# A hybrid scan and convolution layer: the scan's levels 1 to 3 multiplied in one visit, levels 4 to 6 in the last, and convolution operands stored in one run per partition

## The chip, the cores and the metric

The kernel runs on one core of one Trainium2 chip. The metric is the device time of one execution in microseconds (us); the kernel before takes 2150.0 us, the median of three runs (2148.01 to 2152.14). A core has TensorE (PE, with its weight loads PEld), VectorE (DVE), ScalarE (ACT), GpSimd (POOL) and SyncE (SP), which here only issues DMAs. Each engine works through its own queue in order, and engines wait for one another by semaphores.

## What is computed

One layer over 2048 tokens of width 1024, with 256 context tokens ahead of it. A normalised input is multiplied by one large matrix. Part of the result feeds eight heads of a gated linear recurrence that runs in both directions, part a gated convolution of width three along rows of 64 tokens; both are joined and multiplied by an output matrix.

```python
def chunk_scan(q, k, v, logf, s0):
    # S_t = diag(f_t) S_{t-1} + k_t v_t^T,  o_t = S_t^T q_t
    ...
    attn = jnp.einsum('bhtk,bhsk,bhtsk->bhts', qc, kc, decay)
    o = einsum(attn, vc) + einsum(qc * jnp.exp(bcum), S)
...
p = h @ w_in[l]
o, _, _ = bidir_scan(q, kf, kb, v, gf, gb, s_f, s_b)
y_hg = hgrn_out(o, p[..., 4 * HG_WIDTH:HG_COLS], hg_onorm_w[l], x.dtype)
y_cv = conv_branch(p[..., HG_COLS:], conv_w[l], grid=True)
y = jnp.concatenate([y_hg, y_cv], axis=-1) @ w_out[l]
x = x + gate[:, None] * y
```

`decay` is the product of the gates f between two tokens of a chunk.

## The kernel before

**Wide products.** Every large product is done with f16 pairs (a high and a low part, three matmuls for one) and by Strassen's scheme in Winograd's form, `seven`: seven half-size products with operands named B11, T1, T2, B21, T3, B22, T4. Their matmuls are lines 930 to 932. One such product for one stretch of tokens is a "unit". In the head stage a unit covers 512 tokens and its matmuls have 256 columns; in the pair stage, where convolution blocks 1 to 7 are computed, a unit covers 1024 tokens and its matmuls have 512 columns.

**Stages in order.** First the input is normalised (to about 100 us). Then 32 windows follow, eight heads by four token groups of 512, each with two or three units (until about 1265 us). Four windows of the first convolution block come next, then 14 windows of the pair stage (from about 1340 us), and last the output product (from about 1845 us).

**The scan.** The projections of one window are scanned in the next; the scan of one head and group is a "segment" (`Seg`), so there are 32. Q and K hold queries and keys for both directions. The attention within a chunk of 128 is built by levels: at level `lev`, tokens are in blocks of B = 2^lev, and only pairs of neighbouring blocks are multiplied. After each level `update` multiplies K (`level_k`, line 485) and Q (`level_q`, line 492) in place by the gates' block products, on VectorE, and `level_tot` (line 498) makes the block products of the next level in the tile `tot`.

A level's product needs K and Q as they were at that level, the halves of both directions mixed. `mixed` (line 601) copies K into a tile `km` of its own, on ScalarE, before K is changed; `km` has three buffers. Q is read in place, through a strided view (`mix`), or copied to a tile `qm` by GpSimd (`held`, line 608); `qm` has one buffer. So the levels go in pairs: `levels(0)` multiplies the diagonal and level 0; `held(1)` keeps level 1 and `levels(2)` multiplies levels 1 and 2 in one visit of TensorE; `held(3)` and `levels(4)` do 3 and 4; `held(5)` and `level6` do 5 and 6. A visit's products land in one tile of PSUM (A). For levels 0 to 4 VectorE chooses the entries that belong to the level with a masked copy into `Ac` (line 639, five per segment); levels 5 and 6 fill whole blocks of A, which ScalarE copies out (line 661), and GpSimd puts `Ac` into its diagonal (line 665). These products are f32, 32 (at levels 5 and 6, 64) columns wide, 16 for each level, and TensorE does each in two passes, so the trace shows 32 for each.

**What sets the order.** The steps of a segment are spread over the ticks of the next window's units: each step has a weight (`PACE`: values 0.65, begin 1.0, levels 1.55, held 1.1, level6 2.64, keys 1.0, states 2.0, out 0.53), the weights are summed over the chain, and a step is issued when its share of the window's ticks has passed (`merge_steps`, `run`). On top of that the framework's planner orders each engine's queue, with costs of its own: an instruction that it takes to be late can be passed by a later one. The trace shows, for instance, K's first levels on VectorE ahead of Q's level 0. On TensorE the small products stand between the units' wide matmuls, and what is behind a waiting one waits too.

**The convolution's operands.** The operands of the pair stage, 14 tiles `C0` and `C1` of [128, 4, 2, 512] f16, are loaded once from DRAM by `load_C` (line 991), each in two halves of 256 columns; SyncE issues these between about 1282 and 1368 us. Later the same tiles take the output matrix's operands (`wo_home`, `load_wo`).

Of the kernel before, what the change touches and what calls it, by code (L numbers as in the profile page):

```python
# [60 lines left out]
def hybrid_layer(ctx: ExitStack, tc, x, cx, w_ada, b_ada, w_in, w_out, fnorm_w, small_d, masks, ident_d, sel_d, out):  # L61
# [32 lines left out]
    def pa_t(nm):  # L94
        return pa.tile([P, 512], F32, tag="pa", name=nm)
# [4 lines left out]
    def ring(nm):  # L100
        return rp.tile([P, GW], F32, tag="ring", name=nm)
# [375 lines left out]
    def mix(t, n, B, np_, off=0):  # L477
        return sub(t, off, [[2 * B, np_], [n + B, 2], [1, B]])
# [28 lines left out]
    class Seg:  # L507
# [71 lines left out]
                    lambda put: put(s.q[:, HW:]))  # L579

        def start_levels(s):
            s.tot = ring(f"tot_{s.nm}") if s.small else scp.tile([P, 2 * GW], F32, tag="tot", name=f"tot_{s.nm}",
                                                                 bufs=1)
            s.tot7 = tot7_tile(f"tot7_{s.nm}")
            s.cur, s.off = s.f, 0
# [5 lines left out]

        def begin_levels(s):
            s.start_levels()
            s.mixed(0)

        def mixed(s, lev):
# [6 lines left out]
        def held(s, lev):  # L603

            B = 1 << lev
            n = s.n
            qm = scp.tile([P, GW], F32, tag="qm", name=f"qm{lev}_{s.nm}", bufs=1)
            G.tensor_copy(sub(qm, 0, [[2 * B, n // (2 * B)], [B, 2], [1, B]]), mix(s.qf, n, B, n // (2 * B)))  # L608
            s.kept = s.km, qm
            s.update(lev)  # L610

        def update(s, lev):
# [7 lines left out]
        def levels(s, lev):  # L620

            n = s.n
            B = 1 << lev
            k1, q1 = s.kept if lev else (s.ks, s.q)
            pt = pa_t(f"A{lev}_{s.nm}")
            for i in range(2):
                for ch in range(NCH):
                    for j in range(P // SB):
                        o = ch * P + j * SB
                        c = i * P + ch * SB  # L630
                        PE.matmul(pt[j * SB:(j + 1) * SB, c:c + SB], (s.km if i else k1)[:, o:o + SB],
                                  mix(s.qf, n, B, SB // (2 * B), o) if i else q1[:, o:o + SB], start=True, stop=True)
            s.update(lev)
            at = [pt[:, i * P:(i + 1) * P].rearrange("p (c t) -> p c t", c=NCH) for i in range(2)]
            if lev == 0:
                s.Ac = scp.tile([P, NCH, SB], F32, tag="Ac", name=f"Ac_{s.nm}")
                S.activation(s.Ac, at[0], AF.Copy)
            for i in range(2) if lev else (1,):
                V.copy_predicated(s.Ac, sub(mask, (lev - 1 + i) * SB, [[0, NCH], [1, SB]]), at[i])

        def level6(s):

            n = s.n
            km, qm = s.kept
            s.pt = pa_t(f"A5_{s.nm}")
            for ch in range(NCH):
                for j in range(P // SB):
# [4 lines left out]
            for ch in range(NCH):  # L652
                for j in range(P // SB):
# [61 lines left out]
    def scan_steps(h, s):  # L715
# [25 lines left out]

        return ([paced("values", s.value_turn), paced("begin", s.begin_levels)]
                + [paced("levels", lambda: s.levels(0)), paced("held", lambda: s.held(1)),
                   paced("levels", lambda: s.levels(2)), paced("held", lambda: s.held(3)),
                   paced("levels", lambda: s.levels(4))]
                + [paced("held", lambda: s.held(5)), paced("level6", s.level6), paced("keys", s.key_turn), paced("states", states),
                   paced("out", outp)])

    ymax = cp.tile([P, 3 * HEADS, NG], F32, name="ymax")
# [309 lines left out]

    def wo_home(name, hl):  # L1060
        i = 2 * OPS.index(name) + hl
        return C[i // 7][OPS[i % 7]]

    def wo_at(name, hl, k):
        return wo_home(name, hl)[:, k // 2, k % 2, :]

    def load_wo(lo_, hi_):

        for i in range(lo_, hi_):
            SY.dma_start(wo_home(OPS[i // 2], i % 2).rearrange("p a k n -> p (a k) n"), Wd[OPS[i // 2]][:, i % 2])  # L1070

    Gr = dp.tile([P, GW], F32, name="Gr", tag="Gr")

# [379 lines left out]
    def run(wi, units, steps):  # L1453
# [20 lines left out]
        for un, (wk, kind, i, fn) in enumerate(units):  # L1474
# [36 lines left out]
            elif kind == "pair":  # L1511
                def pair_step(o, last_unit=ui == len(uses) - 1):
                    tick(2)
                    if o and last_unit and o != OPS[6]:
                        load_wo(7 + OPS.index(o), 8 + OPS.index(o))

                seven(w.ops.get, lambda o, hl, k, i=i: C[i][o][:, k, hl, :], HK, GW, f"{ui}", pair_step,
                      w.sx[:, 0:1], ring, retire, *fn(w))
            else:
                def step(o, final=final):  # L1520
# [164 lines left out]
```

## Time and profile before

| | before |
|---|---|
| median of three runs | 2150.0 us |
| the profiled execution | 2151.83 us |
| its span on the engines | 2150.1 us |
| TensorE busy | 2073.2 us, 96% |
| VectorE busy | 1645.8 us, 77% |
| ScalarE busy | 1192.2 us, 55% |
| GpSimd busy | 191.8 us, 9% |
| mean granted TensorE clock | 0.994 |

In the lines of the profile, a group shows line, engine, operation, output and inputs by the program's names, then the count, total busy time, mean duration and the idle time of the engine before such instructions with what ended it. A row of the timeline shows start, length, engine, line, operation, names and count. Matmul ends are modelled, so time on TensorE is best read from one start to the next. Names cut short (A, Q, km) stand for all buffers of a kind.

### The profile page before, as it was taken

To read this page: it belongs to the slowest core of one execution; us is meant where nothing else is said; L and a number is where in the kernel's file an instruction comes from. 1 tells how busy PE (TensorE), PEld (TensorE's weight loads), DVE (VectorE), ACT (ScalarE), POOL (GpSimd) and SP (SyncE) were. 2 spreads that over 40 slices of the span, in tenths; PEclk is the share of its full clock that TensorE was granted. 3 is DMA by queue.
4 is the path that set the end of the run, shared out by engine and by line. 5 is a ranking of instruction groups with operands and counts; after the bars stand their busy time and mean duration, and the time that the engine had idled before them with its cause. 6 is when DMAs were issued, how large, how long until landed. Compare 5 with 4: busy or idle time off the path is not lost.

```text
span 2150.1 us, 53050 instructions
## 1 busy us (share of the span) xinstructions
PE 2073.2 (96%) x22111; PEld 1466.0 (68%) x22111; DVE 1645.8 (77%) x3413; ACT 1192.2 (55%) x2406; POOL 191.8 (9%) x272
## 2 busy tenths in 40 slices
PE   5988999999999999999999999999999999999998
PEld 2877878888888888888888887444444444444443
DVE  6787988878778787788687887678778656687775
ACT  7965666757567666576676654354445423333332
POOL 0121111111111110111110100000000000000000
PEclk9999999999999999999999999999999999999999
DMA  9567533442344233424543458933442105642421
GB/s 356 191 207 265 178 126 134 137 158 72 114 129 146 97 114 109 153 81 142 194 131 127 130 165 260 285 108 110 134 149 93 54 23 196 206 143 92 137 79 59
DMA packets 185798, 311.02 MB, mean 145 GB/s; under 512 B 13010, under 2 KB 114770, under 8 KB 183764
## 3 DMA queue, kind: packets, MB, share of 16 engines
q1 hardware_dynamic: 183396, 303.68, 42.9%
q8 instruction: 173, 2.83, 0.5%
q10 hardware_dynamic: 2160, 3.93, 0.5%
q14 instruction: 69, 0.57, 0.1%
HBM read 240.19 MB, written 67.37 MB: 143 GB/s over the span
## 4 chain that ended last, share of the span: by engine, by line
PE 65%; DVE 18%; ACT 7%; DMA 4%; issue 3%; POOL 1%; SPq 0%; POOLq 0%; ACTq 0%; DVEq 0%
PE sa L930 8%; PE sa L932 8%; PE sa L931 8%; PE sb L930 4%; PE sb L932 4%; PE sb L931 4%; PE sa_o L930 2%; PE sa_o L931 2%; PE sa_o L932 2%; DVE Q L492 2%; PE sc L930 2%; PE sc L931 2%; PE sc L932 2%; DVE K L485 2%; PE T L681 2%
## 5 line engine op out<-in xcount | busy, mean ns | idle before, releaser
L931 PEld LDWEIGHTS <-e_p 128*128 128x128 f16 x1332 | 130.4, 98 | 59.8 <-issue 10.3
L930 PEld LDWEIGHTS <-e_p 128*128 128x128 f16 x1332 | 130.4, 98 | 54.0 <-issue 1.1
L601 ACT ACTIVATE km<-K 128x512 f32<-128x512 f32 x192 | 129.6, 675 | 67.2 <-DVE K L485 61.1
L932 PEld LDWEIGHTS <-e_p 128*128 128x128 f16 x1332 | 130.3, 98 | 51.4
L485 DVE TENSOR_TENSOR K<-K,tot 128x512 f32<-128x512 f32 x192 | 132.2, 689 | 42.9 <-ACT km L601 25.3
L492 DVE TENSOR_TENSOR Q<-Q,tot 128x512 f32<-128x512 f32 x192 | 132.5, 690 | 34.9 <-POOL qm L608 19.5
L608 POOL COPY qm<-Q 128x512 f32<-128x512 f32 x96 | 80.8, 842 | 794.4 <-DVE Q L492 778.7
L931 PEld LDWEIGHTS <-whib_p 128*128 128x128 f16 x888 | 86.9, 98 | 42.1 <-issue 8.8
L930 PEld LDWEIGHTS <-whib_p 128*128 128x128 f16 x888 | 86.8, 98 | 36.7 <-issue 0.8
L930 PEld LDWEIGHTS <-whia_p 128*128 128x128 f16 x888 | 87.0, 98 | 35.7 <-DMA hop3B<-Hd3B 2.3
L932 PEld LDWEIGHTS <-wloa_p 128*128 128x128 f16 x888 | 87.0, 98 | 34.2
L931 PEld LDWEIGHTS <-whia_p 128*128 128x128 f16 x888 | 87.0, 98 | 33.9 <-issue 1.5
L932 PEld LDWEIGHTS <-wlob_p 128*128 128x128 f16 x888 | 86.8, 98 | 34.0
L157 ACT ACTIVATE e_p<-ws_p,sc_p 128x512 f16<-128x512 f32 x108 | 77.5, 718 | 54.9 <-DVE ws_p L444 42.0
L665 POOL COPY A<-Ac 32x128 f32<-32x128 f32 x128 | 77.2, 603 | 128.3 <-ACT A L661 110.6
L853 ACT ACTIVATE cv<-c,small 128x512 f32<-128x512 f32 (+1 forms) x36 | 24.2, 673 | 106.8 <-DVE c L871 61.1
L937 ACT ACTIVATE u<-sa,sx_w 128x256 f32<-128x256 f32 (+1 forms) x111 | 58.1, 524 | 43.5 <-PE sa L932 34.7
L937 ACT ACTIVATE p<-sa,sx_w 128x256 f32<-128x256 f32 (+1 forms) x111 | 57.4, 517 | 39.9 <-PE sa L932 39.8
L158 DVE SCALAR_TENSOR_TENSOR e_p<-ws_p,sc_p,e_p 128x512 f16<-128x512 f32 x108 | 79.4, 750 | 0.0
L409 ACT ACTIVATE junk<-ws_p 128x1024 f16<-128x1024 f32 x72 | 75.7, 1052 | 6.5 <-DMA ws_p<-in_w_in 6.3
L1596 POOL TENSOR_TENSOR x_o<-x_o,fw 128x512 f32<-128x512 f32 x1 | 1.3, 1262 | 868.0 <-ACT junk L1587 868.0
L937 ACT ACTIVATE p<-sb,sx_w 128x256 f32<-128x256 f32 (+1 forms) x111 | 57.8, 521 | 30.8 <-PE sb L932 28.0
(858 smaller groups left out, 7036.3 us busy)
## 6 DMA issues: line engine op xcount, KB each, us to landing
ws_p<-in_w_in SPq DMA_DIRECT2D x72, 512.0 KB, 4.3
y_o<-yT SPq DMA_DIRECT2D x32, 512.0 KB, 4.3
xt_x<-in_x SPq DMA_DIRECT2D x16, 512.0 KB, 6.2
wa<-in_w_ada SPq DMA_DIRECT2D x16, 512.0 KB, 10.2
Gd<-zs SPq DMA_DIRECT2D x32, 256.0 KB, 2.7
sg<-Gd SPq DMA_DIRECT2D x32, 256.0 KB, 4.4
wos<-in_w_out SPq DMA_DIRECT2D x32, 256.0 KB, 5.0
yT<-y SPq DMA_DIRECT2D x32, 256.0 KB, 2.9
```

The source lines that it names most:

```text
L157: S.activation(hi, src, AF.Copy, scale=st[:, 0:1])
L158: V.scalar_tensor_tensor(lo, src, st[:, 0:1], hi, ALU.mult, ALU.subtract)
L409: S.activation(junk.rearrange("p (k n) -> p k n", k=KT), stage[i], AF.Abs, accum_out=r)
L485: V.tensor_tensor(m, m, sub(cur, nb + 1, [[2, np_], [-(nb + 1), 2], [0, B]]), ALU.mult)
L492: V.tensor_tensor(m, m, sub(cur, 1, [[2, np_], [nb - 1, 2], [0, B]]), ALU.mult)
L601: S.activation(sub(s.km, 0, [[2 * B, n // (2 * B)], [B, 2], [1, B]]), mix(s.K, n, B, n // (2 * B)), AF.Copy)
L608: G.tensor_copy(sub(qm, 0, [[2 * B, n // (2 * B)], [B, 2], [1, B]]), mix(s.qf, n, B, n // (2 * B)))
L665: G.tensor_copy(A3[js, :, js], s.Ac[js])
L930: PE.matmul(ps, hi[:, k], rh, start=start and k == 0, stop=False, skip_group_check=not start)
L931: PE.matmul(ps, hi[:, k], right(name, 1, k), start=False, stop=False, skip_group_check=not start)
L932: PE.matmul(ps, lo[:, k], rh, start=False, stop=k == nk - 1, skip_group_check=not start)
L937: last_keep.append(S.activation(r, ps, AF.Copy, scale=sx))
```

## The change

The levels are kept and multiplied in other groups. `s.kept` becomes a list: levels 1 and 2 are both held (`held(1)`, `held(2)`) and multiplied with level 3 in `levels(3)`; levels 4 and 5 are held and multiplied in `level6` with level 6. So `qm` gets a second buffer and is copied at levels 1, 2, 4 and 5. Masked copies are three after level 3 and one, of level 4, after level 6's `update`. The tile `tot` is 768 wide instead of 1024: from level 2 on it is written from its start again. The chain has two steps `levels` and four `held` instead of three and three.

The tiles `C` become [128, 2, 4, 2, 256], so that each half that a DMA loads is one run of 4 KB in a partition instead of eight of 512 bytes, and a matmul of the pair stage reads its 512 columns as two runs of 256. The output matrix's operands keep their place in these tiles, by a view of the whole tile as one run.

```diff
@@ level_tot, start_levels, begin_levels
-        return dst, off + nb
+        return dst, off + nb if lev != 1 else 0
...
-            s.tot = ... scp.tile([P, 2 * GW], F32, tag="tot", ...)
+            s.tot = ... scp.tile([P, GW + HW], F32, tag="tot", ...)
...
             s.start_levels()
+            s.kept = [(s.ks, s.q)]
             s.mixed(0)
@@ held
-            qm = scp.tile([P, GW], F32, tag="qm", name=f"qm{lev}_{s.nm}", bufs=1)
+            qm = scp.tile([P, GW], F32, tag="qm", name=f"qm{lev}_{s.nm}", bufs=2)
...
-            s.kept = s.km, qm
+            s.kept.append((s.km, qm))
             s.update(lev)
@@ levels becomes products, choose and levels
+        def products(s, kept, nm, lev=0):
             n = s.n
             B = 1 << lev
-            k1, q1 = s.kept if lev else (s.ks, s.q)
-            pt = pa_t(f"A{lev}_{s.nm}")
-            for i in range(2):
+            pt = pa_t(nm)
+            for i, (k_, q_) in enumerate(kept):
                 for ch in range(NCH):
                     for j in range(P // SB):
                         o = ch * P + j * SB
                         c = i * P + ch * SB
-                        PE.matmul(pt[j * SB:(j + 1) * SB, c:c + SB], (s.km if i else k1)[:, o:o + SB],
-                                  mix(s.qf, n, B, SB // (2 * B), o) if i else q1[:, o:o + SB], start=True, stop=True)
+                        PE.matmul(pt[j * SB:(j + 1) * SB, c:c + SB], k_[:, o:o + SB],
+                                  mix(s.qf, n, B, SB // (2 * B), o) if q_ is None else q_[:, o:o + SB],
+                                  start=True, stop=True)
+            return [pt[:, i * P:(i + 1) * P].rearrange("p (c t) -> p c t", c=NCH) for i in range(len(kept))]
+
+        def choose(s, at, lev):
+            for i, a_ in enumerate(at):
+                V.copy_predicated(s.Ac, sub(mask, (lev + i) * SB, [[0, NCH], [1, SB]]), a_)
+
+        def levels(s, lev):
+            at = s.products(s.kept + [(s.km, None)], f"A{lev}_{s.nm}", lev)
+            s.kept = []
             s.update(lev)
             if lev == 0:
                 s.Ac = scp.tile([P, NCH, SB], F32, tag="Ac", name=f"Ac_{s.nm}")
-                S.activation(s.Ac, at[0], AF.Copy)
-            for i in range(2) if lev else (1,):
-                V.copy_predicated(s.Ac, sub(mask, (lev - 1 + i) * SB, [[0, NCH], [1, SB]]), at[i])
+                S.activation(s.Ac, at.pop(0), AF.Copy)
+            s.choose(at, lev + 1 - len(at))
@@ level6
-            km, qm = s.kept
+            at = s.products(s.kept[:1], f"A4_{s.nm}")
+            km, qm = s.kept[1]
...
             s.update(6)
+            s.choose(at, 4)
             s.A = ring(f"A_{s.nm}")
@@ scan_steps
-                   paced("levels", lambda: s.levels(2)), paced("held", lambda: s.held(3)),
-                   paced("levels", lambda: s.levels(4))]
-                + [paced("held", lambda: s.held(5)), paced("level6", s.level6), ...
+                   paced("held", lambda: s.held(2)), paced("levels", lambda: s.levels(3)),
+                   paced("held", lambda: s.held(4)), paced("held", lambda: s.held(5))]
+                + [paced("level6", s.level6), ...
@@ load_C, wo_home, the pair stage's reads
-                C[tp][o] = (pool or ext.cr).tile([P, HK, 2, GW], F16, name=f"C{tp}{o}")
-            SY.dma_start(C[tp][o][:, :, :, j * HW:(j + 1) * HW], Hd[2 * tp + j][o])
+                C[tp][o] = (pool or ext.cr).tile([P, 2, HK, 2, HW], F16, name=f"C{tp}{o}")
+            SY.dma_start(C[tp][o][:, j], Hd[2 * tp + j][o])
...
-        return C[i // 7][OPS[i % 7]]
+        return C[i // 7][OPS[i % 7]].rearrange("p j k l n -> p (j k l n)").rearrange("p (k n) -> p k n", n=GW)
...
-                seven(w.ops.get, lambda o, hl, k, i=i: C[i][o][:, k, hl, :], HK, GW, ...
+                seven(w.ops.get, lambda o, hl, k, i=i: C[i][o][:, :, k, hl, :], HK, GW, ...
```

More of the change, by code (lines that the diff above doesn't have):

```diff
@@ L581, in start_levels @@
         def start_levels(s):
-            s.tot = ring(f"tot_{s.nm}") if s.small else scp.tile([P, 2 * GW], F32, tag="tot", name=f"tot_{s.nm}",
+            s.tot = ring(f"tot_{s.nm}") if s.small else scp.tile([P, GW + HW], F32, tag="tot", name=f"tot_{s.nm}",
                                                                  bufs=1)
@@ L743, in scan_steps @@
                 + [paced("levels", lambda: s.levels(0)), paced("held", lambda: s.held(1)),
[L744 to L746 removed]
+                   paced("held", lambda: s.held(2)), paced("levels", lambda: s.levels(3)),
+                   paced("held", lambda: s.held(4)), paced("held", lambda: s.held(5))]
+                + [paced("level6", s.level6), paced("keys", s.key_turn), paced("states", states),
                    paced("out", outp)])
@@ L1061, in wo_home @@
         i = 2 * OPS.index(name) + hl
-        return C[i // 7][OPS[i % 7]]
+        return C[i // 7][OPS[i % 7]].rearrange("p j k l n -> p (j k l n)").rearrange("p (k n) -> p k n", n=GW)
     def wo_at(name, hl, k):
-        return wo_home(name, hl)[:, k // 2, k % 2, :]
+        return wo_home(name, hl)[:, k, :]
     def load_wo(lo_, hi_):
         for i in range(lo_, hi_):
-            SY.dma_start(wo_home(OPS[i // 2], i % 2).rearrange("p a k n -> p (a k) n"), Wd[OPS[i // 2]][:, i % 2])
+            SY.dma_start(wo_home(OPS[i // 2], i % 2), Wd[OPS[i // 2]][:, i % 2])
     Gr = dp.tile([P, GW], F32, name="Gr", tag="Gr")
@@ L1515, in pair_step @@
                         load_wo(7 + OPS.index(o), 8 + OPS.index(o))
-                seven(w.ops.get, lambda o, hl, k, i=i: C[i][o][:, k, hl, :], HK, GW, f"{ui}", pair_step,
+                seven(w.ops.get, lambda o, hl, k, i=i: C[i][o][:, :, k, hl, :], HK, GW, f"{ui}", pair_step,
                       w.sx[:, 0:1], ring, retire, *fn(w))
```

2 lines of the change are left out of this document (removed).

## The prediction

> **What bounds the kernel now.** I read the page's head first, then the stretches of the run, then what TensorE waited for.
>
> ```profile
> span 2150.1 us, 53050 instructions
> PE 2073.2 (96%) x22111; PEld 1466.0 (68%) x22111; DVE 1645.8 (77%) x3413; ACT 1192.2 (55%) x2406; POOL 191.8 (9%) x272
> ...
> PE 65%; DVE 18%; ACT 7%; DMA 4%; issue 3%; POOL 1%; SPq 0%; POOLq 0%; ACTq 0%; DVEq 0%
> ```
>
> Stretch, length, and busy time (instructions) of PE, PEld, DVE, ACT, POOL; then clock, DMA share, GB/s:
>
> ```profile
> 100.00:320.00 220.00, 199.40 (x3040) 168.89 (x3044) 188.23 (x422) 141.58 (x299) 44.22 (x60) 0.99 0.58 192
> 320.00:1265.00 945.00, 926.43 (x14184) 819.49 (x14173) 754.95 (x1661) 619.39 (x1393) 129.75 (x186) 1.00 0.39 128
> 1265.00:1400.00 135.00, 133.27 (x930) 91.31 (x928) 90.84 (x192) 56.44 (x131) 0.00 (x0) 1.00 0.82 255
> 1400.00:2150.00 750.00, 739.17 (x3427) 333.53 (x3425) 538.95 (x946) 293.21 (x446) 4.16 (x3) 0.99 0.35 114
> ```
>
> The scan lies in the first two stretches. From 320 us on TensorE is busy 98% of the time (926.43 of 945) and VectorE 80%; before that 91% and 86%. So TensorE bounds, and a gain must come either from what TensorE executes or from its waits. Those waits at the scan's level products (A), on the whole page, and then from 320 us on (total, times, longest):
>
> ```profile
> PE A L631 <- POOL qm L608: 9.7, 13, 2.7
> PE A L631 <- DVE Q L492: 3.1, 9, 0.9
> PE A L650 <- POOL qm L608: 2.7, 2, 1.5
> ```
>
> ```profile
> PE A L631 <- POOL qm L608: 6.1, 7, 2.7
> PE A L631 <- DVE Q L492: 1.9, 7, 0.3
> ```
>
> Together 15.5 us, of which 8.0 us after 320 us. That is the stall there is to win; everything else must come from TensorE's own work.
>
> **Term 1, one visit fewer per segment.** A "visit" is a break in TensorE's stream of wide f16 matmuls to do the small level products. Before, a segment has four (A0, A2, A4, and level 6); after, three (A0, A3, and level 6 with A4 in front). The number of small matmuls stays: 32+32+32+16+16 before, 32+48+16+16+16 after (each counts twice in the trace, as two passes). What changes is how often the stream is broken. Visits in the trace: first the end of one at level 2 (602.32) and a whole one at level 4 with two blocks, then one with a single block, then the start of one at level 6:
>
> ```profile
> 602.32 0.28 PE L930 MATMUL sc<-hop14B,whia_p 128*128 128x256 f16 x1
> ...
> 604.84 0.27 PE L932 MATMUL sb<-hop14B,e_p 128*128 128x256 f16 x1
> 605.04 0.46 PE L631 MATMUL A<-qm,km 128*32 128x32 f32 x32
> 605.32 0.49 PE L631 MATMUL A<-Q,km 128*32 128x32 f32 x32
> 605.74 0.28 PE L930 MATMUL sb<-hop14B,e_p 128*128 128x256 f16 x1
> 605.86 0.27 PE L931 MATMUL sb<-hop14B,e_p 128*128 128x256 f16 x1
> ```
>
> ```profile
> 286.64 0.27 PE L931 MATMUL sb<-hop5T,whib_p 128*128 128x256 f16 x1
> 286.75 0.27 PE L932 MATMUL sb<-hop5T,wlob_p 128*128 128x256 f16 x1
> 286.95 0.46 PE L631 MATMUL A<-Q,km 128*32 128x32 f32 x32
> 287.35 0.28 PE L930 MATMUL sb<-hop5T,whib_p 128*128 128x256 f16 x1
> ```
>
> ```profile
> 609.23 0.65 PE L650 MATMUL A<-qm,km 128*32 128x64 f32 x32
> ```
>
> From the wide matmul before to the wide matmul after: 605.74-604.84 = 0.90 us with two blocks, 287.35-286.75 = 0.60 with one. A block costs 0.30, and 0.60-0.30 = 0.30 is the break itself; the stream's own step is 0.11 (286.75-286.64), so a break costs 0.19 us beyond it. One break fewer in each of 32 segments: 32 x 0.19 = **6.1 us** off TensorE. I take 5.8, since some visits are already cut in two by the planner (the single block above is one) and some will be cut again. Bounds: 0 if the 48-matmul visit is always cut in two, 6.1 if never.
>
> **Term 2, the stalls.** Level products are fed by a chain that alternates engines: VectorE scales Q at a level, GpSimd copies the old Q out (qm) before the next level's scaling overwrites it. The piece of the chain of waits that ends in a stalled visit at level 2 (start, length, what):
>
> ```profile
> 598.89 1.04 DVE Q L492
> ...
> 600.04 1.11 POOL qm L608
> 601.18 0.70 DVE Q L492
> 601.93 0.46 PE A L631 x32
> ```
>
> Level 0's scaling ends at 599.93, qm of level 1 is done at 601.15, level 1's scaling at 601.88, and then TensorE can do its second block. The change puts another copy and another scaling into this chain ahead of the visit (qm and Q of level 2), and moves the visit later. Both are to be priced.
>
> *What the chain gains in length:* 0.11 to the copy, the copy, 0.03, scaling 0.70, and the copy is 0.61 to 1.10 us:
>
> ```profile
> 599.95 0.68 DVE L485 TENSOR_TENSOR K<-K,tot 128x512 f32<-128x512 f32 x1
> 600.04 1.10 POOL L608 COPY qm<-Q 128x512 f32<-128x512 f32 x1 [15.59 <-DVE Q L492]
> ...
> 603.27 0.48 DVE L941 SCALAR_TENSOR_TENSOR f<-sc,sx_w,p 128x256 f32<-128x256 f32 x1
> 603.28 0.61 POOL L608 COPY qm<-Q 128x512 f32<-128x512 f32 x1 [2.14 <-DVE Q L492]
> ```
>
> So 1.45 to 1.94 us.
>
> Of the two prices, the copy took 0.49 us more where it ran into a VectorE multiply of two SBUF tensors (599.95 to 600.63) than where VectorE read PSUM. The Trainium skill, SBUF — State Buffer, section "SBUF: two separate sides", says that GpSimd and VectorE share one pair of ports as an exclusive lock, taken by a VectorE instruction with two SBUF inputs against a GpSimd one that reads SBUF, whichever starts first, while the other blocks. That speaks against this change, which adds 32 such copies beside exactly such multiplies, and these two rows agree with it.
>
> *What the visit gains in distance:* the step weights of a segment sum to 15.77 before (0.65+1+3x1.55+3x1.1+2.64+1+2+0.53) and 15.32 after. Level 3's visit comes 1.1 weights after where level 2's was. Between two visits lie 1.55+1.1 = 2.65 weights. The level-2 visit ended at 602.32, so level 4's at 605.04 came 2.72 us later, or 1.03 us per weight; level 6's at 609.23 came 3.5 us after 605.74, or 1.32. So 1.1 x (15.77/15.32) x 1.03 to 1.32 = 1.17 to 1.49 us, and the block that needs the newest Q is now the third, not the second (0.30 more): 1.47 to 1.79 us. This is a window with two units; with three units the weights are longer in time and the distance wins.
>
> 1.45 to 1.94 against 1.47 to 1.79: level 3 is about as late as level 2 was, better by 0.34 or worse by 0.47 us a segment. What goes is level 4 as a place to wait. At level 6 the new chain after level 3's visit is three scalings and two copies with their gaps, 3x0.70+2x(0.61 to 1.10)+0.3 = 3.6 to 4.6 us, against a distance of 3.75 x 1.03 x (1.03 to 1.32) = 4.0 to 5.1 plus the A4 block and the first half of level 6 that run ahead of the newest Q (0.30+0.47): covered. I take **-2 us** for the stalls, since the balance at level 3 is near zero and one waiting place is gone. Bounds: -15.5 (all waits of the rows above go) and +15.0 (0.47 us in each of 32 segments).
>
> **Terms that I put at nothing.** GpSimd: 96 copies become 128, 32 x (0.61 to 1.10) = 20 to 35 us on an engine busy 9%; their cost is in the chain above, nowhere else. VectorE: five masked copies per segment before (1+2+2) and five after (1+3+1), and all scalings stay; the smaller tot tile is rewritten by VectorE in its own order, so no wait is added. New waits: km of level 4 goes to a buffer that level 3's visit reads, so ScalarE's copy stands behind that visit; level 4's K scaling on VectorE waits for it, and ScalarE's evacuations of p1, p5 and u2 queue behind it. Those belong to wide products that TensorE does after the visit, so they were not due before; without that cover the price is one block, 0.30 x 32 = 9.6 us, which lies inside the range. The masked copy of level 4 moves behind level 6's products, and GpSimd's four copies of Ac into A behind it: 0.3 us later, needed only at "out", 5.64 weights (some 6 us) on.
>
> The convolutions' operands: 28 loads whose 512-byte pieces (1,024 a load) become 4 KB pieces. The loads' landing times, a load of the same size that already lands as one run (hop), and the matmuls that use the result (last column: idle before them):
>
> ```profile
> C1B<-Hd2B SPq DMA_DIRECT2D x3, 512.0 KB, 7.0
> ...
> hop35T<-Hd3T SPq DMA_DIRECT2D x3, 512.0 KB, 6.9
> ```
>
> ```profile
> L930 PE MATMUL sa<-C0T,e_p 128*128 128x512 f16 x112 | 42.5, 379 | 0.3
> ```
>
> TensorE idled 0.3 us before these and 1.7 us in all of 1265 to 1400 us (135.00-133.27), so earlier landings have nothing to give: 0, and at most -1.7. In exchange, 14 windows x 2 units x 84 = 2352 matmuls read their 512 columns as two runs of 256. No two-run wide matmul is in the trace. Each unit has 7 products x 4 x 3 = 84. Nearest: Q's blocks above read their 32 columns as two runs of 16 (level 4 mixes halves), and the lone one takes 0.40 us from start to next wide matmul, as the Q block after qm does within 0.02 (605.74-605.32 = 0.42): a break costs 0.02 us over 32 passes at most, 0.6 ns each, x 2352 = 1.5 us. I take 0.
>
> **Sum.** -5.8-2 = -7.8 us. The profiled execution took 2151.83 us (span 2150.1 and 1.7 around it), 1.8 above the median shown, 2150.0; from that execution it would be 2144.0, on the median **2142 us**.
>
> **The rivals.**
> 1. *The stalls go too (2130 us).* With two waiting places instead of three and VectorE spared one wait for TensorE per segment, most of the 15.5 us goes: 2150-5.8-14. For it: 7 of 13 waits on qm are in the steady part. Against it: the longer chain.
> 2. *No change (2149 us).* Either the planner, which thinks an operand late, cuts level 3's visit in two, so that no break is saved, or the breaks are saved and stalls of the same size come back at level 3. For it: lone blocks exist now (286.95). Against it: most visits in the steady part are whole.
> 3. *Slower (2159 us).* The chain through GpSimd decides at level 3: each added copy runs into a VectorE multiply and takes 1.10, so each segment is 0.47 us later: +15.0-5.8 = +9.2. It decides wherever the visit of level 2 had less than 0.47 us to spare; the 13 waits on qm show that this is so in a good part of the segments, not in all. By the lock rule of the Trainium skill (SBUF — State Buffer) this would be the rule rather than the exception; the 0.61 copy above shows that the outcome hangs on what VectorE does at that moment.
> 4. *The layout costs.* If two runs cost a matmul more than I take, the pair stage (from 1340 us on) grows, by 1.5 us at the bound: 2143.5 us, not enough to decide.
>
> **How the numbers follow.** About 0.2%, 4.3 us, is what a measurement here can tell from no change. The forecast (2131 to 2148) has 0.56, rival 1 0.09, rival 2 0.20, rival 3 with anything else slower 0.15. Of the forecast's 0.56 some 0.06 lies within 4.3 us. Faster 0.50+0.09+0.03 of rival 2 = 0.62; same 0.06+0.17 = 0.23; slower 0.15. The range reaches from rival 1's 2130 down one us to 2129, and up to 2156, which leaves out the far half of rival 3.
>
> **What would show it.** Right: blocks of A in visits of 96 passes at level 3, three breaks a segment; waits of the level products on qm and Q at 10 to 16 us; qm copies x128; wide C matmuls still 379 ns, and packets under 2 KB down by 28 x 1,024 = 28,672 from the 114,770 of this row:
>
> ```profile
> DMA packets 185798, 311.02 MB, mean 145 GB/s; under 512 B 13010, under 2 KB 114770, under 8 KB 183764
> ```
>
> The forecast is wrong if level-3 visits come cut in two with wide matmuls between (rival 2), if waits on qm grow past 20 us (rival 3), or if the pair stage's length of 750 us after 1400 changes by more than 2 us.

## The result, and the profile after

The kernel after takes 2185.2 us, the median of four runs (2182.3 to 2186.5), against 2149.0 us for the kernel before, the median of four runs (2146.9 to 2152.1). The ratio is 1.0164, with a 95% interval of 1.0152 to 1.0176: 36 us slower, where 2142 us and a gain were predicted. The profiled execution took 2186.1 us.

The page's head, the DMA row and the shares of the chain of waits, after:

```profile
span 2184.3 us, 53097 instructions
PE 2075.0 (95%) x22111; PEld 1471.5 (67%) x22111; DVE 1658.0 (76%) x3413; ACT 1195.7 (55%) x2406; POOL 198.4 (9%) x304
DMA packets 160710, 311.02 MB, mean 142 GB/s; under 512 B 13010, under 2 KB 86098, under 8 KB 158676
PE 59%; DVE 22%; ACT 9%; DMA 4%; issue 4%; POOL 2%; SPq 0%; POOLq 0%; ACTq 0%; DVEq 0%
```

TensorE has as much to do as before (2075.0 us; before 2073.2), so the time is not in its work. VectorE is 12.2 us busier with the same 3413 instructions, and its share of the chain goes from 18 to 22%. Where the time goes shows when one head's four windows are set side by side, from the first product of level 0 in each to that of the next. Two windows of the fifth head, before and then after, in the columns of the prediction's stretches; the first row of each pair is the head's third window, the second its fourth:

```profile
771.50:809.10 37.60, 37.30 (x563) 33.10 (x563) 33.14 (x69) 24.82 (x46) 5.59 (x7) 1.00 0.20 65
809.10:856.00 46.90, 46.25 (x645) 41.18 (x647) 35.71 (x83) 28.82 (x64) 4.57 (x7) 1.00 0.38 119
```

```profile
788.60:829.50 40.90, 38.60 (x563) 33.76 (x562) 33.91 (x69) 24.95 (x46) 4.49 (x8) 0.96 0.18 60
829.50:876.70 47.20, 46.01 (x641) 41.16 (x640) 35.62 (x83) 28.46 (x64) 5.69 (x8) 1.00 0.38 119
```

The third window grows by 3.3 us, the fourth by 0.3, and the granted clock in the third is 0.96. The head's first window grows by 0.8 us (30.06 to 30.86), its second shrinks by 0.6 (29.20 to 28.59). VectorE was busy 88% of the third window already before (33.14 of 37.60), against 72 to 76% of the other three. What TensorE waited for on the whole page (total, times, longest), first before and then after:

```profile
PE sa L930 <- ACT u L937: 3.6, 12, 0.6
PE sa L930 <- DVE f L941: 3.1, 7, 1.2
```

```profile
PE sa L941 <- ACT u L948: 26.5, 21, 3.5
PE sa L941 <- DVE f L952: 8.4, 7, 1.4
...
PE A L660 <- POOL qm L609: 5.7, 3, 2.8
...
PE sa L941 <- ACT p L948: 3.6, 3, 2.4
...
PE A L631 <- DVE Q L492: 2.7, 5, 1.4
...
PE A L667 <- DVE Q L492: 1.2, 2, 0.6
...
PE A L631 <- POOL qm L609: 0.8, 1, 0.8
```

The level products wait less than before: 5.7+2.7+1.2+0.8 = 10.4 us against 15.5. The wide products wait more: 26.5 us for `u`, the evacuation of a finished product that ScalarE makes, against 3.6. (For `f`, VectorE's evacuation, it is 8.4 against 6.1, since before another 3.0 us stood at products named `sb`.) One such wait, in the third window of the third head, read from the timeline: VectorE and GpSimd, then ScalarE, then TensorE.

```profile
502.90 0.29 DVE L638 COPY_PREDICATED Ac<-mask,A 128x128 f32<-128x128 uint8 x1
503.14 1.13 DVE L485 TENSOR_TENSOR K<-K,tot 128x512 f32<-128x512 f32 x1
...
505.19 0.14 DVE L151 TENSOR_SCALAR sc_p<-ss_p 128x1 int32<-128x1 int32 x1
...
505.44 0.14 DVE L153 TENSOR_SCALAR sc_p<-sc_p 128x1 int32<-128x1 int32 x1
```

```profile
503.11 0.61 POOL L609 COPY qm<-Q 128x512 f32<-128x512 f32 x1 [7.37 <-DVE Q L492]
```

```profile
504.89 0.46 ACT L948 ACTIVATE p<-sb,sx_w 128x256 f32<-128x256 f32 x1
505.24 0.85 ACT L602 ACTIVATE km<-K 128x512 f32<-128x512 f32 x1
505.99 1.14 ACT L157 ACTIVATE whia_p<-ws_p,sc_p 128x1024 f16<-128x1024 f32 x1
507.03 0.46 ACT L948 ACTIVATE u<-sa,sx_w 128x256 f32<-128x256 f32 x1
```

```profile
503.81 0.27 PE L943 MATMUL sa<-hop11T,e_p 128*128 128x256 f16 x1
...
505.12 0.27 PE L943 MATMUL sc<-hop11B,wloa_p 128*128 128x256 f16 x1
507.54 0.27 PE L941 MATMUL sa<-hop11T,e_p 128*128 128x256 f16 x1 [2.14 <-ACT u L948]
507.65 0.37 PE L942 MATMUL sa<-hop11T,e_p 128*128 128x256 f16 x1
```

The same place before, the end of the same product on TensorE and its `u` on ScalarE:

```profile
495.07 0.27 PE L932 MATMUL sa<-hop11T,e_p 128*128 128x256 f16 x1
```

```profile
496.42 0.46 ACT L937 ACTIVATE u<-sa,sx_w 128x256 f32<-128x256 f32 x1
```

Three things stand in it. `u` is queued on ScalarE behind a copy `km`, of the next segment's level 0, and behind `whia_p`, the high part of the next weights. ScalarE is not waiting there: it goes from `p` to `u` without a gap, but `u` begins 3.22 us after the last matmul of its product (503.81 to 507.03), where it was 1.35 us before (495.07 to 496.42). Second, `whia_p` also needs the scale `sc_p`, which VectorE comes to only at 505.19, after what level 3's visit let loose. It is ready at 505.58, 0.41 us ahead of `whia_p`'s turn at 505.99: not what holds `u` up here, but the next limit close behind it. In seven heads a wait of 2.10 to 2.36 us stands at this place, 15.4 us of the 26.5, each time with ScalarE busy from `p` through `km` and `whia_p` to `u`. Third, K's scaling takes 1.13 us there, not 0.68: GpSimd's copy began 0.03 us ahead of it and takes its usual 0.61. In the prediction's rows it was the other way round: K's scaling began 0.09 us ahead (599.95 against 600.04), kept its 0.68, and the copy took 1.10. Over the whole page, in the groups' rows (count, busy, mean ns), before and after:

```profile
L485 DVE TENSOR_TENSOR K<-K,tot 128x512 f32<-128x512 f32 x192 | 132.2, 689 | 42.9 <-ACT km L601 25.3
...
L608 POOL COPY qm<-Q 128x512 f32<-128x512 f32 x96 | 80.8, 842 | 794.4 <-DVE Q L492 778.7
```

```profile
L485 DVE TENSOR_TENSOR K<-K,tot 128x512 f32<-128x512 f32 x192 | 143.4, 747 | 28.3 <-ACT km L602 18.6
...
L609 POOL COPY qm<-Q 128x512 f32<-128x512 f32 x128 | 90.5, 707 | 802.7 <-DVE Q L492 788.4
```

The loser has changed: GpSimd, with 91% of its time free, waited before; VectorE waits now, 143.4-132.2 = 11.2 us in all. Instruction by instruction, 35 of the 192 scalings after took over 0.78 us with a copy `qm` begun ahead of them, and one before; these 35 hold 10.7 us of the difference. Copies over 0.80 us fell from 40 of 96 to 20 of 128. Both pairs agree with what the Trainium skill, SBUF — State Buffer, section "SBUF: two separate sides", says of the lock: whichever of the two starts first holds the pair for its whole instruction.

### The profile page after: what moved, and what is told of

The parts are those of the page before. It is cut to its first block, busy times and chain, and to the rows that moved or that the text cites. A ratio compares the mean times of both kernels' runs of the same rounds, so it can differ in the third digit from the quotient of the medians.

```text
span 2184.3 us, 53097 instructions
## 1 busy us (share of the span) xinstructions
PE 2075.0 (95%) x22111; PEld 1471.5 (67%) x22111; DVE 1658.0 (76%) x3413; ACT 1195.7 (55%) x2406; POOL 198.4 (9%) x304
## 4 chain that ended last, share of the span: by engine, by line
PE 59%; DVE 22%; ACT 9%; DMA 4%; issue 4%; POOL 2%; SPq 0%; POOLq 0%; ACTq 0%; DVEq 0%
PE sa L941 7%; PE sa L943 7%; PE sa L942 7%; DVE Q L492 4%; PE sb L941 3%; PE sb L943 3%; PE sb L942 3%; DVE K L485 3%; PE sa_o L941 2%; PE sa_o L943 2%; PE sa_o L942 2%; PE sc L943 2%; PE sc L942 2%; PE sc L941 2%; PE T L692 2%
## 5 line engine op out<-in xcount | busy, mean ns | idle before, releaser
L485 DVE TENSOR_TENSOR K<-K,tot 128x512 f32<-128x512 f32 x192 | 143.4, 747 | 28.3 <-ACT km L602 18.6
L609 POOL COPY qm<-Q 128x512 f32<-128x512 f32 x128 | 90.5, 707 | 802.7 <-DVE Q L492 788.4
L676 POOL COPY A<-Ac 32x128 f32<-32x128 f32 x128 | 72.4, 566 | 139.8 <-ACT A L672 126.9
L157 ACT ACTIVATE hiS_o<-y_o,sc_y 128x1024 f16<-128x1024 f32 x32 | 36.8, 1149 | 72.7 <-PE sa_o L942 32.1
```

Source lines behind the costliest of these rows:

```text
L157: S.activation(hi, src, AF.Copy, scale=st[:, 0:1])
L485: V.tensor_tensor(m, m, sub(cur, nb + 1, [[2, np_], [-(nb + 1), 2], [0, B]]), ALU.mult)
L676: G.tensor_copy(A3[js, :, js], s.Ac[js])
```

## The experiments

**Which part of the change.** The scan's part alone, and the layout of C alone:

```diff
 scan_only: level_tot to scan_steps as after; load_C, wo_home, load_wo and the pair stage's reads as before
 c_only:    the reverse
```

> The scan part alone, with the operands C stored as before. Theory A (the loss in the head stage is ScalarE: the copies km of levels 4 and 5 and of the next segment's level 0 are all released by level 3's visit, and the evacuation u of a wide product, which TensorE waits for, is queued behind them): the head stage stays 30 us longer, so 2179 to 2186 us; waits of sa on ACT u near 26 us. In the changed kernel a stall of 2.8 us and a slow clock behind it lie at the end of the pair stage (4.3 us): if they come from the layout of C this run gives 2181, if from the scan's other order 2185. Rival B (the layout of C costs most of it, through the DMAs): below 2160 us.

> The layout of C alone, with the scan as before. Theory A: 2149 us, or 2153 if the stall at the end of the pair stage belongs to the layout; wide C matmuls stay 216 ns from start to start. Rival B: above 2170 us.

Measured: the scan alone 2181.9 us, ratio 1.0152 (1.0137 to 1.0167); the layout alone 2148.2 us, 0.9996 (0.9987 to 1.0006). The layout is worth nothing either way, and the regrouping alone loses 33 of the 36 us; its interval overlaps that of the whole change.

**Which half of the regrouping.** Level 3 into the first visit, with level 4 in a visit of its own; and level 3 in a visit of its own, with level 4 in the last:

```diff
 three_123: visits 0 | 1,2,3 | 4 | 5,6
 three_456: visits 0 | 1,2 | 3 | 4,5,6
```

> The changed kernel with levels 1 to 3 in one visit, but level 4 multiplied in a visit of its own, so that 5 and 6 go together as before: four visits, three copies qm a segment. Theory A: level 3's visit still releases the buffers of km 4, km 5 and the next km 0 together, so the loss stays: 2172 to 2190 us, and waits on ACT u over 15 us. Rival C (the longer chain from GpSimd's copies to VectorE and back decides, at level 6 as much as at level 3): one qm copy a segment fewer and none ahead of level 4, so about half the loss, 2160 to 2170, with waits on qm in place of those on ACT u.

> The changed kernel with levels 1 and 2 in one visit as before, level 3 in a visit of its own, and 4 and 5 kept for level 6: four visits, three copies qm a segment. Theory A: level 2's visit releases the buffers of km 4 and km 5 as in the kernel before, and only the next km 0 comes early, so most of the loss is gone: 2148 to 2162 us, waits on ACT u below 8 us. Rival C: two qm copies in a row stand ahead of level 6, so it loses as much as the other half, 2160 to 2170 us.

Measured: 2167.5 us, 1.0086 (1.0071 to 1.0101), and 2155.9 us, 1.0030 (1.0018 to 1.0042). Both have as many visits as the kernel before. TensorE's waits, first with levels 1 to 3 together, then with 4 to 6:

```profile
PE sa L939 <- ACT u L946: 13.9, 18, 2.5
```

```profile
PE sa L941 <- ACT u L948: 7.3, 12, 1.4
```

18.5 and 6.9 us make 25 of the 36: the halves add up to less than the whole. In the profile of the second, most is one stall at the end of the pair stage, where SyncE's read-back of y waited 5.0 us for the last write of y to DRAM (2.1 before); the same is in the profile after (5.1), and not in those of `scan_only` (2.3), `three_123` (2.1) or `c_only`. In these profiles it comes and goes with that write's landing, and goes with neither part of the change.

**First theory: ScalarE's copies of K.** Level 3's visit reads all three `km` buffers, so the copies for levels 4 and 5 and the next segment's level 0 come free at once, ahead of `u` in ScalarE's queue. Take them out of that stretch:

```diff
 km45_pool, in mixed():
-            S.activation(km, mix(K), Copy)
+            (G.tensor_copy(km, mix(K)) if lev in (4, 5) else S.activation(km, mix(K), Copy))
 km0_late, in begin_levels():
-            s.mixed(0)
+            behind(lambda: s.mixed(0))      # after the last evacuation issued so far
 km45_km0: both
```

> The kernel after, with the copies km of levels 4 and 5 made by GpSimd (64 of 192), the rest as it is. Theory A (ScalarE's in-order queue: level 3's visit frees three km buffers at once, so the copies of levels 4 and 5 and of the next segment's level 0 are queued ahead of the evacuation of u, and TensorE waits for it): waits of the wide matmuls on ACT u fall from 26.5 us to below 10, the time comes to 2155 to 2172 us. Rival D (VectorE's chain decides: the scalings of levels 3 to 6 come late, by the wait for the visit and by the port that VectorE shares with GpSimd): 64 more GpSimd copies run into VectorE multiplies, waits on DVE f grow past 10 us, time 2185 us or more.

> The kernel after, with the next segment's copy km of level 0 issued behind the retiring of the unit before it, so that it stands behind u in ScalarE's queue; the copies of levels 4 and 5 stay on ScalarE. Theory A: one of three copies (0.85 of some 2.1 us) leaves the stretch ahead of u; waits on ACT u fall from 26.5 to between 10 and 20 us, time 2165 to 2180 us. Rival D: waits on ACT u may fall but the time stays within 4 us of 2185, since VectorE is as late as before.

> Both edits: no km copy stands ahead of u in the queue. Theory A: waits on ACT u at 3 to 6 us as in the kernel before, time 2145 to 2165 us, 2143 if nothing else was lost by the regrouping. Rival D: as with GpSimd's copies alone, 2180 us or more, with waits on DVE f.

Measured: 2196.9 us, 1.0231 (1.0216 to 1.0246); 2190.5, 1.0200 (1.0183 to 1.0217); 2200.5, 1.0244 (1.0229 to 1.0259). All slower than the kernel after. With both edits no copy of K stands ahead of `u`, yet TensorE waits longer for it; the row of `km45_km0`, its `whia_p` in the third window of the third head with what ScalarE idled for, and K's scalings in `km45_pool`:

```profile
PE sa L945 <- ACT u L952: 36.4, 23, 3.8
```

```profile
514.23 1.15 ACT L157 ACTIVATE whia_p<-ws_p,sc_p 128x1024 f16<-128x1024 f32 x1 [1.36 <-DVE sc_p L152]
```

```profile
L485 DVE TENSOR_TENSOR K<-K,tot 128x512 f32<-128x512 f32 x192 | 145.6, 758 | 33.9 <-ACT km L606 12.0
```

The theory is not enough. In the kernel after, the copy does stand ahead of `u`, but the second limit, `sc_p`, falls away only 0.41 us before the first. With the copies gone ScalarE idles for `sc_p`: 1.36 us here, and 0.22 in `km0_late`, where TensorE's wait at this place is still 2.13 us. Giving GpSimd 64 more copies made K's scalings longer still, 758 ns.

**Second theory: one place, the scale of the next weights.** Begin the weights' preparation earlier (`wait1`), move level 3's visit later (`pause2`), do both (`p2w1`), and as the reverse, begin the preparation later in the kernel before (`bwait8`):

```diff
 wait1, in retire():            -  next_w(wk[2], 4)    +  next_w(wk[2], 1)
 pause2, in the chain of steps:
-   paced("held", held(2)), paced("levels", levels(3)),
+   paced("held", held(2)), paced(2.0, lambda: None), paced("levels", levels(3)),
 p2w1: both
 bwait8, in the kernel before:  -  next_w(wk[2], 4)    +  next_w(wk[2], 8)
```

> The kernel after, with the preparation of the next weights begun one tick after a unit retires instead of four; the scan's steps stay where they are. Theory E (the scale of the next weights, sc_p, stands in VectorE's in-order queue behind the work that level 3's visit lets loose: two scalings of K, two of Q and three masked copies; whia_p waits for sc_p on ScalarE, u is queued behind whia_p, and TensorE waits for u): at the first weights of a head one K, one Q and a masked copy less stand ahead of the scale, its delay behind the matmul ss_p falls from 2.6 us to below 2, waits on ACT u fall from 26.5 to below 18, time 2158 to 2176 us. Rival F (VectorE and ScalarE are late everywhere because the regrouping bunches the scan's work, whatever the weights do): within 5 us of 2185.

> The kernel after, with an empty step of weight 2.0 ahead of level 3's visit, so that the visit and what follows it come about 2 us later in the window. Theory E: only one Q scaling and one masked copy stand ahead of the scale at the first weights of a head, its delay falls below 1 us, waits on ACT u below 12 us, time 2150 to 2168 us, with some of it given back by waits of level 6's products on qm and Q, which now have 2 us less. Rival F: the same bunch stands elsewhere, 2180 us or more.

> Both edits: the visit 2 weights later and the weights' preparation three ticks earlier, so that no scan work stands ahead of the scale at the first weights of a head. Theory E: its delay is some 0.2 us as in the kernel before, waits on ACT u 3 to 8 us, time 2143 to 2160 us. Rival F: 2175 us or more.

> The kernel before, its scan untouched, with the preparation of the next weights begun eight ticks after a unit retires instead of four; two scalings of K, two of Q and two masked copies then stand ahead of the scale in VectorE's queue. Theory E: the loss comes without the regrouping: the scale's delay rises from 0.2 to above 1.5 us, waits on ACT u from 3.6 to above 15 us, time 2160 to 2185 us. Rival F: 2145 to 2153 us, as the kernel before.

Measured: 2191.9 us, 1.0193 (1.0176 to 1.0210); 2185.2, 1.0163 (1.0147 to 1.0178); 2193.2, 1.0202 (1.0185 to 1.0219); 2157.8, 1.0037 (1.0024 to 1.0050). From the matmul `ss_p` (L145) to `sc_p` (L151) it is 0.2 us before and 2.6 after at a head's first weights; `wait1` leaves 2.8 and `bwait8` makes only 0.4, so neither of them set the condition that it was to test (and of the 8 us of `bwait8` only 1.2 lie ahead of the first matmul with C). `pause2` (0.6, but 3.1 in the last two heads) and `p2w1` (0.4) did, and there the theory fails: the waits for `u` do fall, to 18.9 and 16.1 us (in five heads the wait at this place to 0.7 and 0.6 us), but others rise. The waits on `qm` and on ScalarE's `kT`, of `pause2`:

```profile
PE sa L941 <- ACT u L948: 18.9, 18, 3.0
...
PE A L660 <- POOL qm L609: 10.4, 15, 2.1
...
PE T L692 <- ACT kT L685: 4.6, 5, 1.2
```

A stall taken away at this place comes back at the next.

**Third theory: the buffers, and fourth: the lock.** A fourth `km` buffer frees level 4's copy and scaling from level 3's visit; its space comes out of the ring of temporaries, which gets a control. In the kernel before, two buffers instead of three bring the same tie in. And ScalarE instead of GpSimd makes the copies `qm`, in the kernel after and then, as a control, in the kernel before:

```diff
 a_km4r9:  km bufs=3 -> 4, ring bufs=10 -> 9
 a_r9:     ring bufs=10 -> 9
 b_km2:    the kernel before with km bufs=3 -> 2
 a_qmact, b_qmact, in held():
-            G.tensor_copy(qm, mix(Q))
+            S.activation(qm, mix(Q), Copy)
```

> The kernel after with a fourth buffer for km (its 2 KB a partition are taken from the ring of temporaries, 9 instead of 10), so that the copy of K for level 4, and with it K's scaling at level 4, needs not wait for level 3's visit. Theory B (level 3's visit holds all three km buffers and Q, so that K's scalings of levels 4 and 5 and Q's of 3 to 5 all come behind it in a bunch on VectorE, and whatever VectorE owes to the wide products then is late): one of five scalings leaves the bunch, stalls of the steady part fall from 72 us to 45 to 65 us, time 2155 to 2178 us. Theory L (the lock between GpSimd's copies and VectorE's scalings makes VectorE longer, 1658 us busy against 1646 before): no change, 2181 to 2189 us.

> Control for the fourth km buffer: the kernel after with the ring of temporaries at 9 alone. Both theories: 2181 to 2190 us, that is no change; a loss here is to be taken off the other run.

> The kernel before, its groups of levels untouched, with two km buffers instead of three, so that the copies of K for levels 3 and 4 both wait for the visit of level 2. Theory B: the loss comes without the regrouping: 2160 to 2190 us, with waits of the wide matmuls on ACT u and DVE f above 15 us in all. Theory L: 2145 to 2154 us, as the kernel before, as GpSimd's copies are the same.

> The kernel after with the copies qm made by ScalarE instead of GpSimd, so that no copy of GpSimd locks a scaling out (128 x some 0.65 = 83 us more on ScalarE, 55 to 59% busy). Theory L: K's scalings fall from 747 to 690 ns, VectorE's busy time to 1645 us or below, time 2150 to 2172 us. Theory B: VectorE's time falls as well, but the bunch stays, and ScalarE's queue is longer: 2180 us or more.

> The kernel before with the copies qm made by ScalarE instead of GpSimd: the control for the same edit on the kernel after, which gave 17 us (2185 to 2168, K's scalings 747 to 690 ns). Theory L2 (the lock costs VectorE only in the kernel after, where GpSimd's copy starts first; in the kernel before K's scalings take 689 ns and GpSimd's copies 842 ns, so GpSimd is the one that waits): little to gain, 2140 to 2152 us, K's scalings 685 to 690 ns; some gain from the waits on qm (12.4 us), which become shorter. Rival M (the edit helps either kernel alike, by a shorter copy, so it says nothing on the regrouping): 2130 to 2136 us.

Measured: the fourth buffer 2191.1 us, 1.0191 (1.0170 to 1.0213), its control 2184.7, 1.0166 (1.0145 to 1.0187): no gain. Two buffers before: 2161.3, 1.0052 (1.0033 to 1.0070), which is in the range expected but by other waits: 9.1 us of the level products on `km` itself, and only 5.1 on `u`. So the tie through the `km` buffers alone does not explain the loss. In `a_km4r9` K's scalings take 139.5 us, 3.9 less than after, without any gain in time; ScalarE idles 0.53 us for `sc_p` at the same place.

The kernel after with ScalarE's copies takes 2168.2 us, 1.0086 (1.0063 to 1.0109): 17 of the 36 us are gone. The kernel before with the same edit takes 2154.6, 1.0029 (1.0017 to 1.0040): 6 us slower. In its profile, which is only 1.9 us longer than that of before, the first matmul with C starts 0.4 us earlier, so there the scan has lost nothing. First the group of K's scalings and the wait for `u` after with the edit, then the group before with it:

```profile
L485 DVE TENSOR_TENSOR K<-K,tot 128x512 f32<-128x512 f32 x192 | 132.4, 690 | 32.5 <-ACT km L602 25.6
```

```profile
PE sa L941 <- ACT u L948: 24.9, 29, 2.2
```

```profile
L485 DVE TENSOR_TENSOR K<-K,tot 128x512 f32<-128x512 f32 x192 | 131.9, 687 | 39.9 <-ACT km L601 31.7 <-PE A L657 8.0
```

After, the scalings fall from 747 to 690 ns; before, they go from 689 to 687, since there VectorE lost nothing, while ScalarE has 50 us more to do (1192.2 to 1242.7). The waits for `f` fall alike (8.4 to 1.9 us after, 6.1 to 2.0 before); those for `u` fall from 26.5 to 24.9 after and rise from 3.6 to 10.8 before. So the edit gains only in the kernel where VectorE was the one locked out. That moving the copies off GpSimd brings the kernel after 17 us net is shown; that all of it comes through the 11.2 us of longer scalings, and none through the other order of the queues, is argued, and `a_km4r9` speaks against a plain sum.

**What the rest is.** With the lock away, the two ideas of before were tried once more: the visit later, and the masked copies of levels 1 to 3 issued after level 5's step:

```diff
 q_pause2:      a_qmact with pause2's step
 q_masks_late:  a_qmact, choose() of levels 1 to 3 moved from levels(3) to the end of held(5)
```

> The kernel after with qm copied by ScalarE and an empty step of weight 2.0 ahead of level 3's visit. Theory E2 (what is left after the lock is taken away, some 19 us, is the scale of the next weights standing behind the bunch that level 3's visit lets loose, at one place in each head): its delay falls from 2.2 to below 1 us, waits on ACT u from 24.9 to below 15 us, time 2148 to 2162 us. Rival F2 (VectorE's and ScalarE's queues have no slack in the third window of a head, so a stall taken away there comes back at the next wait): 2163 us or more.

> The kernel after with qm copied by ScalarE and the masked copies of levels 1 to 3 issued after level 5's step instead of behind the visit. Theory E2: up to 0.75 us (three masked copies) less stand ahead of the scale at the first weights of a head, and 0.75 us less ahead of what follows the visit in each of 32 segments; time 2156 to 2165 us. Rival F2: the masked copies come later but must come before the segment's end; 2165 to 2172 us.

Measured: 2176.5 us, 1.0128 (1.0114 to 1.0142), and 2164.0, 1.0069 (1.0054 to 1.0084). The later visit costs 8 us more than it brings. The later masked copies come out 4 us lower, which the two intervals (this, and 1.0063 to 1.0109 without) do not tell from no change. No version with the regrouping reaches the kernel before, and none beats it.

## Why the prediction was wrong

**The step that failed** is "Terms that I put at nothing". It named the mechanism: ScalarE's copy of level 4 stands behind the visit, VectorE's K scaling waits for it, and "ScalarE's evacuations of p1, p5 and u2 queue behind it". It then said that these "belong to wide products that TensorE does after the visit, so they were not due before", and that without this cover the price is one block, 9.6 us. The cover is not there in a head's third window: in seven heads `u` is due, and ScalarE comes to it 2.10 to 2.36 us late, behind a copy of K and `whia_p`. VectorE was busy 88% of that window before. Its row was not read, since the prediction took the stretch as a whole, 80%. The price was wrong as well: TensorE waits not for one block but for ScalarE's queue with VectorE's close behind it, 26.5 us for `u` (3.6 before) and 8.4 for `f` (6.1 before).

**The second part of that step** is VectorE itself, also put at nothing ("all scalings stay"). They stay in number, but K's took 11.2 us more. The lock was in the prediction, with both rows, but only as a price for GpSimd's copy (0.61 to 1.10 us), to be felt at the waits on `qm`. That the same collision can cost VectorE, if the copy begins first, was not priced. The rule of the Trainium skill that it cited, SBUF — State Buffer, section "SBUF: two separate sides", allows for either engine to start first and the other to wait.

**Rival 3**, slower at 2159 us, had the right sign for the wrong place: it put the loss on the chain through GpSimd, with waits on `qm` past 20 us. They fell from 12.4 to 5.7+0.8 = 6.5 us.

**What held.** Term 1: a visit less per segment. The start of the wide matmul ahead of a visit and of the one behind it, for level 3 and for level 6 after, then for level 6 before:

```profile
499.10 0.27 PE L943 MATMUL sa<-hop11T,wlob_p 128*128 128x256 f16 x1
499.30 0.75 PE L631 MATMUL A<-qm,km 128*32 128x32 f32 x63
...
500.29 0.28 PE L941 MATMUL sa<-hop11T,whib_p 128*128 128x256 f16 x1
```

```profile
255.53 0.27 PE L943 MATMUL sa<-hop3B,wloa_p 128*128 128x256 f16 x1
...
257.06 0.28 PE L941 MATMUL sb<-hop3T,whib_p 128*128 128x256 f16 x1
```

```profile
609.02 0.27 PE L932 MATMUL sa<-hop14T,wlob_p 128*128 128x256 f16 x1
...
610.26 0.28 PE L930 MATMUL sb<-hop14T,whib_p 128*128 128x256 f16 x1
```

After, 1.19+1.53 = 2.72 us; before, 0.90+0.90+1.24 = 3.04. Less the stream's own step of 0.11, this is 0.21 us a segment, 6.7 us, against 0.19 and 6.1. Level 3's visits come whole in 30 of 32 segments. Term 2: the waits at the level products are 10.4 us, inside the 10 to 16 expected, 5 us less than before where 2 were taken. The copies `qm` are 128. The packets under 2 KB fell by exactly 28,672, and the wide matmuls of C read their two runs in the same time, row after:

```profile
L941 PE MATMUL sa<-C0T,e_p 128*128 128x512 f16 x112 | 42.4, 379 | 0.3
```

From the first matmul with C to the end the profile grew by 4.2 us, past the 2 us set as a sign against the forecast, but by the stall on y's write, which the layout alone does not have. So both gains came, some 12 us by these rows, and were lost four times over in terms that stood at nothing.

**What stays open.** Of 36 us, 17 went with GpSimd's copies. The other 19 are in the main waits of the wide products in the scan's windows, most of them on `u`: 24.9 us remain, against 3.6 before. Part of that may belong to the edit itself, since `b_qmact` has 10.8 us of them. Another part of the 36 is the granted clock (last section). That they come with the regrouping, and most with level 3 in the first visit (18.5 us alone, though that kernel has the copies on GpSimd as well), is shown. That the queues of VectorE and ScalarE have no slack there, so that work bunched behind one later visit is late wherever it is put, fits `km0_late`, `wait1`, `pause2`, `p2w1`, `a_km4r9` and `q_pause2`, which only moved the stalls or made them longer; but no run took that bunch away, so it is argued and not shown.

## What to carry to other kernels

Before putting "queued behind, but not due" at nothing, find the window in which the engine named has the least slack, not its share of a long stretch: 80% over a stage hid 88% in every fourth window. Where two engines take turns on something exclusive, price the collision on both of them, and ask which one the change lets start first; the engine with spare time should be the one that waits. When a saving comes from joining visits, list what the joined visit frees at one moment, and who is behind it in each queue.

## What the runs showed of the hardware that was not expected

A stall of TensorE of some 2 us can cost more than its length. After the wait that ended at 507.54 the next matmuls start 0.21 us apart, not 0.11:

```profile
508.03 0.42 PE L941 MATMUL sa<-hop11T,e_p 128*128 128x256 f16 x1
508.24 0.42 PE L942 MATMUL sa<-hop11T,e_p 128*128 128x256 f16 x1
```

This lasts from 507.65 to at least 509.73 us and loses some 1 us. It does not follow every such wait: at the same place of the fourth head TensorE waits 2.13 us, until 655.57, and then steps 0.11. Two stretches of 3.4 us behind these waits, with the granted clock in the third column from the end:

```profile
507.70:511.10 3.40, 3.40 (x68) 2.44 (x70) 2.69 (x6) 2.35 (x4) 0.00 (x0) 0.50 0.00 0
655.50:658.90 3.40, 3.33 (x114) 2.85 (x114) 3.40 (x6) 2.59 (x6) 0.00 (x0) 1.00 0.00 0
```

Of the seven waits of 2.10 to 2.36 us, three were followed by half clock and four were not; what decides it no run here shows. The Trainium skill, TensorE: Matmul & The Clock Gate, section "Part 1: The HAM clock gate (the "warmup" mystery)", ties the half clock to an idle window of about 3.4 us. Here a gap of 2.42 us from start to start (505.12 to 507.54) was enough once, and one of 2.41 us (653.16 to 655.57) was not. Between 100 and 2100 us the traces hold seven stretches of 3.4 us at half clock after, two before and one in `a_qmact`. The third windows with one (third and fifth head) grew by 3.3 us, those without (fourth and sixth) by 2.7, so by estimate the five more stretches are some 3 us of the 36, and the six fewer in `a_qmact` some 4 of its 17.

The other is the lock: of two instructions that began 0.03 to 0.09 us apart, the later one took 0.45 to 0.49 us longer, whichever engine it was on.
